# Keys, queries and values of a gated delta rule made token-major by VectorE block transposes and scattered stores, with norms taken per half, in a hybrid layer kernel

## The chip, the core and the metric

The kernel runs on one core of one Trainium2 chip. The metric is the device time of one execution in microseconds: the median of three runs, and beside it one profiled execution with its trace. Engines are named as in the profile: PE (TensorE matmuls), PEld (its weight loads), DVE (VectorE), ACT (ScalarE), POOL (GpSimd), SP (the queue that issues all DMAs here).

## The reference

One layer of a hybrid encoder trunk is computed for 2048 prompt tokens and 32 sample tokens, width 1024, in float32. The mixer projects the normalised input and splits the columns: half go through a spatial-gating MLP, half through a gated delta rule with 4 heads of 128. Then follow an output projection, and a feed-forward part with squared ReLU and 4096 hidden channels. What the change touches is this (shortened):

```python
qkv, new_buf = causal_conv(qkv, conv_buf, conv_w)
qkv = jax.nn.silu(qkv).reshape(B, L, 3 * DN_HEADS, DN_HEAD_DIM)
q = l2norm(qkv[:, :, :DN_HEADS]) * (DN_HEAD_DIM ** -0.5)
k = l2norm(qkv[:, :, DN_HEADS:2 * DN_HEADS])
vv = qkv[:, :, 2 * DN_HEADS:].astype(jnp.float32)
...
a = jnp.einsum('bhnid,bhnjd->bhnij', kb, k) * dec_strict
sol = triangular_solve(a + eye, concat([v * beta, kb * exp(gc)]), lower=True, unit_diagonal=True)
attn = jnp.einsum('bhnid,bhnjd->bhnij', q, k) * dec_incl
kg = k * jnp.exp(gc[..., -1:] - gc)[..., None]
...
v_new = u_i - w_i @ s
o = qg_i @ s + attn_i @ v_new
s = s * gl_i + kg_i.T @ v_new
```

## The kernel before, in words

The kernel keeps activations channel-major: 128 channels on the partitions, tokens along the columns. It does not write its instructions in a fixed order. Each operation is recorded with its engine, an estimated cost and what it reads and writes (`Program.op`), and `Program.schedule` then simulates the engines and writes a static list for each one. Among the operations that are ready an engine takes the one with the best priority (the recurrence first, then the inverse, the local work, evictions, and the large projections last), and by due time after that. A PSUM bank is a ring of its own for each kind of work: "g" for projections, "L" for local work, "C" for the recurrence, "B" for the inverse, "M" for the rest. On the chip each engine runs its list strictly in order, with semaphores. All DMAs go through SP, in order too.

The tokens are split into two halves of 1024 and 1056 columns (the 32 sample tokens are at the end of the second). For each half `mixers` runs these stages, whose matmuls the schedule mixes:

- `v_stage`: the gating MLP's v and the decay and beta columns, token-major; `gates` makes the decays.
- `qkv_tile`, once for each of k, q and v of each head: a projection per group of up to 512 tokens (24 matmuls, three per 128 rows of the contraction, for the split of a float32 in two), a copy of the bank to SBUF, a causal convolution of width 4 (one scaled copy on ACT, three operations on DVE), SiLU, and a store in DRAM: k and q of a head in `kq_d`, v in `v_d`.
- `delta_local`, once per head and half, in four batches of two chunks of 128 tokens. It loads k, q and v, turns each chunk on PE with the identity (line 431: six transposes a batch, into ring "L"), squares k and q out of PSUM on ACT with an accumulator read for the norms, takes a power of -1/2 on POOL, makes small columns from it, multiplies k with k and q (the score products, ring "L") and scales them by the decays. The turned and scaled k and v and the scaled scores go packed to `pk_d`.
- `delta_inv`, once per pair of heads and half: the inverse of the triangular matrices, by a solve on POOL and small matmuls in ring "B".
- `delta_chain`, once per pair: the recurrence over eight chunks of 128 tokens in ring "C". For each batch `load` brings packed k, v, scores, the inverse and k, q channel-major.
- `sample`: the same for the 32 sample tokens of all four heads; its results, like those of `delta_out`, pass through DRAM (`mix_d`).
- `u_stage`: the gating MLP's u.

Then `out_stage` projects the first half, and the second. Its input is loaded from `mix_d` and split in two (BH on ACT, BL on DVE). The feed-forward part follows in three blocks of tokens.

The lines that the page and the views name are those of helpers: L358 `act` (ACT), L373 `tt`, L378 `stt`, L387 `ts` (DVE or POOL), L396 `cp`, L404 the 32x32 block transpose of DVE (the view calls it STREAM_TRANSPOSE; before, it is used in the inverse alone), L411 `dma`, L420 a matmul, L431 a transpose on PE. Names like "s" are slots of SBUF, "L", "g", "C" the rings of banks, "wh" and "wl" the two parts of the weights.

## Time and profile before

| | |
|---|---|
| median of 3 runs | 2304.45 us (2303.17 to 2306.07) |
| profiled execution | 2305.26 us, its span 2303.5 us |
| mean granted TensorE clock | 0.998 |
| DMA, mean over the span | 238 GB/s, 547.32 MB |
| packets under 512 B | 66233 of 358198 |

A row of a group names line, engine, operation, what is written and read, shapes and count; then busy us in total and the mean ns of one instruction, and the idle time of the engine ahead of them with what ended it. A row of the order of time begins with the start and the duration in us from the span's start. Matmuls overlap, so the distance of two starts tells what one costs, rather than its duration. A row of one tile's or line's instructions gives the shortest, median and longest duration in ns.

### The profile page before, as it was taken

To read this page: it belongs to the slowest core of one execution; us is meant where nothing else is said; L and a number is where in the kernel's file an instruction comes from. 1 tells how busy PE (TensorE), PEld (TensorE's weight loads), DVE (VectorE), ACT (ScalarE), POOL (GpSimd) and SP (SyncE) were. 2 spreads that over 40 slices of the span, in tenths; PEclk is the share of its full clock that TensorE was granted. 3 is DMA by queue.
4 is the path that set the end of the run, shared out by engine and by line. 5 is a ranking of instruction groups with operands and counts; after the bars stand their busy time and mean duration, and the time that the engine had idled before them with its cause. 6 is when DMAs were issued, how large, how long until landed. Compare 5 with 4: busy or idle time off the path is not lost.

```text
span 2303.5 us, 45375 instructions
## 1 busy us (share of the span) xinstructions
PE 2280.8 (99%) x15890; PEld 2172.0 (94%) x15890; DVE 1660.0 (72%) x3599; ACT 1208.3 (52%) x2787; POOL 568.0 (25%) x722
## 2 busy tenths in 40 slices
PE   9999999999999999999999999999999999999998
PEld 6877879999999988999999999999999999999998
DVE  7556756677654546589999989876668885666775
ACT  5466656566654434476655546753444564344344
POOL 1123531222413023444445424210001250000001
PEclk9999999999999999999999999999999999999999
DMA  9578877576556857987777787997668797666771
GB/s 330 170 267 285 265 233 234 154 225 206 155 182 197 263 190 226 295 267 265 257 255 263 251 273 242 335 306 246 216 212 265 258 306 230 217 220 216 249 221 54
DMA packets 358198, 547.32 MB, mean 238 GB/s; under 512 B 66233, under 2 KB 182093, under 8 KB 357969
## 3 DMA queue, kind: packets, MB, share of 16 engines
q1 hardware_dynamic: 357968, 544.42, 72.6%
q8 instruction: 125, 2.05, 0.4%
q14 instruction: 105, 0.85, 0.1%
HBM read 390.96 MB, written 153.31 MB: 236 GB/s over the span
## 4 chain that ended last, share of the span: by engine, by line
PE 84%; DVE 6%; DMA 4%; ACT 2%; issue 2%; SPq 1%; POOL 1%; POOLq 0%; DVEq 0%; ACTq 0%
PE f L420 47%; PE g L420 27%; DVE s L373 4%; PE C L420 3%; PE B L420 2%; PE L L420 2%; DVE wl L373 1%; SPq L411 1%; ACT s L358 1%; PE M L420 1%; PE L L431 1%; DMA s<-x_d 1%; POOL s L373 0%; DMA s<-s_d 0%; ACT wh L358 0%
## 5 line engine op out<-in xcount | busy, mean ns | idle before, releaser
L420 PE MATMUL f<-s,wh 128*128 128x348 f32 (+1 forms) x2768 | 662.3, 322 | 1.3 <-DVE s L373 1.3
L358 ACT ACTIVATE s<-s 128x348 f32<-128x348 f32 (+13 forms) x1059 | 491.2, 487 | 326.6 <-DVE s L373 146.8
L420 PEld LDWEIGHTS f<-s,wh 128*128 128x128 f32 x2768 | 481.0, 188 | 3.3 <-DVE s L373 2.8
L373 DVE TENSOR_TENSOR s<-f,s 128x348 f32<-128x348 f32 (+1 forms) x696 | 348.0, 513 | 166.6 <-PE f L420 164.5
L420 PE MATMUL f<-s,wl 128*128 128x348 f32 (+1 forms) x1384 | 444.7, 321 | 0.0
L420 PE MATMUL g<-BH,wh 128*128 128x384 f32 (+2 forms) x1088 | 400.4, 368 | 2.4 <-ACT s L358 1.9
L373 DVE TENSOR_TENSOR s<-s,s 128x348 fp32r<-128x348 f32 (+8 forms) x674 | 353.2, 553 | 41.1 <-ACT s L358 20.5
L420 PE MATMUL g<-BH,wl 128*128 128x384 f32 (+2 forms) x1088 | 381.7, 351 | 0.0
L420 PE MATMUL g<-BL,wh 128*128 128x384 f32 (+2 forms) x1088 | 380.6, 350 | 0.5 <-DVE BL L378 0.5
L420 PE MATMUL f<-BL,wh 128*128 128x348 f32 (+1 forms) x1024 | 330.2, 322 | 0.0
L420 PE MATMUL f<-BH,wh 128*128 128x348 f32 (+1 forms) x1024 | 329.0, 321 | 0.0
L420 PE MATMUL f<-BH,wl 128*128 128x348 f32 (+1 forms) x1024 | 328.6, 321 | 0.0
L373 POOL TENSOR_TENSOR s<-s,s 128x512 f32<-128x512 f32 (+17 forms) x303 | 241.3, 800 | 341.2 <-ACT s L358 138.0
L358 ACT ACTIVATE wh<-s 128x512 fp32r<-128x512 f32 x282 | 176.6, 631 | 226.6 <-PE f L420 180.3
L420 PEld LDWEIGHTS f<-s,wl 128*128 128x128 f32 x1384 | 260.4, 188 | 0.0
L373 DVE TENSOR_TENSOR wl<-s,wh 128x512 fp32r<-128x512 f32 x282 | 217.2, 777 | 37.9 <-ACT wh L358 37.7
L420 PEld LDWEIGHTS g<-BH,wh 128*128 128x128 f32 x1088 | 204.9, 188 | 26.8 <-issue 7.1
L420 PEld LDWEIGHTS g<-BH,wl 128*128 128x128 f32 x1088 | 204.3, 188 | 18.2
L420 PEld LDWEIGHTS g<-BL,wh 128*128 128x128 f32 x1088 | 205.4, 189 | 16.6 <-DVE BL L378 0.8
L378 DVE SCALAR_TENSOR_TENSOR s<-s,s,s 128x256 f32<-128x256 f32 (+4 forms) x314 | 164.1, 544 | 55.3 <-ACT s L358 29.5
L358 ACT ACTIVATE wh<-wr 128x512 fp32r<-128x512 f32 (+2 forms) x159 | 124.3, 783 | 139.6 <-PE f L420 61.0
L420 PEld LDWEIGHTS f<-BL,wh 128*128 128x128 f32 x1024 | 192.3, 188 | 0.4 <-DVE BL L373 0.3
(134 smaller groups left out, 3264.6 us busy)
## 6 DMA issues: line engine op xcount, KB each, us to landing
s<-w_u SPq DMA_DIRECT2D x124, 256.0 KB, 3.6
s<-w_d SPq DMA_DIRECT2D x121, 256.0 KB, 3.9
wh<-su_d SPq DMA_DIRECT2D x114, 256.0 KB, 3.8
wl<-su_d SPq DMA_DIRECT2D x114, 256.0 KB, 4.1
wh<-sd_d SPq DMA_DIRECT2D x100, 256.0 KB, 3.0
wl<-sd_d SPq DMA_DIRECT2D x100, 256.0 KB, 3.8
wr<-w_b SPq DMA_DIRECT2D x36, 512.0 KB, 5.0
s<-adaw SPq DMA_DIRECT2D x32, 512.0 KB, 5.9
```

What stands on the lines that cost most here:

```text
L358: self.p.op(ACT, c, lambda: nc.scalar.activation(out=R(out), in_=R(in_), func=func, **{k: R(v) for k, v in kw.items()}), [out, accum], [in ...
L373: self.p.op(eng, c, lambda: e.tensor_tensor(out=R(out), in0=R(a), in1=R(b), op=op), [out], [a, b])
L378: self.p.op(DVE, c, lambda: nc.vector.scalar_tensor_tensor(out=R(out), in0=R(a), scalar=R(s), in1=R(b), op0=op0, op1=op1), [out], [a, s, b])
L411: self.p.op(DMA, max(500, x), lambda: nc.sync.dma_start(out=R(out), in_=R(in_)), [out], [in_], lat=LAND + b / RATE - max(500, x))
L420: nc.tensor.matmul(R(out), R(l), R(r), **kw)
L431: self.p.op(PE, 114, lambda: nc.tensor.transpose(R(out), R(in_), R(ident)), [out], [in_, ident])
```

## The change

k, q and v are turned on DVE, in `qkv_tile`, once the whole half of a tile has gone through SiLU into one buffer `yo` of 1056 columns. One block transpose turns 32x32 blocks: it reads columns 33 apart, so that a block holds the tokens i*33 + c of 32 channels, and writes contiguous columns to `yt`. For k and v four DMAs (one for each 32 channels) then store the blocks token-major in `kt_d`, as 1056 pieces of 32 elements each. For k and q, `yt` is squared in place on ACT, summed over the 32 channels of each piece on DVE (`sums`), and stored in `ns_d` as partial sums of squares.

`delta_local` loads the four partial sums of k and q of a head's whole half at once, turns them with one transpose on PE (64 rows, ring "B"), adds them, and makes the norm columns for all eight chunks together. The six transposes a batch, the squares with accumulators and the scaled copies of k and v go from there; it stores only the scores. `delta_chain`'s `load` now reads k and v from `kt_d`, 1 KB a token, and scales them in place on ACT with the same columns. The score products still read channel-major k and q. `sample` reads token-major k and v from `kt_d` and its partial sums from `ns_d`.

Beside that, the slabs of weights come in the order k, q, k, q, v, v for each pair of heads; a head's `delta` is called behind its q instead of its v. The first scaled copy of the convolution reads the SBUF copy, not the bank. Ring "g" has three banks, "L" one. The normalisation of the second half's input is given a due time.

```diff
-        self.banks = {"g": [0, 1], "L": [3, 2], "C": [4, 5], "B": [6], "M": [7]}
+        self.banks = {"g": [0, 1, 2], "L": [3], "C": [4, 5], "B": [6], "M": [7]}
...
+            self.p.due = len(self.p.ops) + 300 * (g + 1)
...
-            fm = ["k0", "q0", "v0", "k1", "q1", "v1", "k2", "q2", "v2", "k3", "q3", "v3"]
+            fm = ["k0", "q0", "k1", "q1", "v0", "v1", "k2", "q2", "k3", "q3", "v2", "v3"]
...
-                        if name[0] == "v":
+                        if name[0] == "q":
                             self.delta(hf, int(name[1]))
+                        elif name[0] == "v":
                             due.append(int(name[1]))
...
-            raw, y, yo = self.new("raw"), self.half("y", w), self.half("yo", w)
+            raw, y, yo = self.new("raw"), self.half("y", w), self.yo[:, o : o + w]
...
-            self.act(y, ps, AF.Identity, scale=cw(3))
+            self.act(y, raw[:, 3 : 3 + w], AF.Identity, scale=cw(3))
...
             self.act(yo, y, AF.Silu)
-            self.dma(dst[:, T0[hf] + o : T0[hf] + o + w], yo)
+            if ty < 2:
+                self.dma(self.kq_d[h][:, 1 - ty, T0[hf] + o : T0[hf] + o + w], yo)
+        self.transpose32(self.yt.re("p (c j) -> p c j", j=32), self.yo.re("p (i c) -> p c i", i=32))
+        if ty:
+            for b in range(4):
+                self.dma(self.kt_d[h][hf][:, ty - 1, 32 * b : 32 * b + 32].re("(i c) j -> i c j", i=32), self.yt[32 * b : 32 * b + 32].re("p (c j) -> p c j", j=32), 2 * P * SLOT)
+        if ty < 2:
+            self.act(self.yt, self.yt, AF.Square)
+            part = self.new("sqp")
+            self.sums(part, self.yt.re("p (c j) -> p c j", j=32))
+            self.dma(self.ns_d[h][hf][1 - ty].re("b (i c) -> (b i) c", i=32), part)
...
+        ns, rr = self.new("ssl"), self.new("ssr")
+        self.dma(ns[:64], self.ns_d[h][hf][:, :, :TW[0]].re("x b (c p) -> (x b) c p", p=P))
+        ss, rr = rr[:, :16], rr[:, 16:]
+        pt = self.bank("B")
+        self.tr(pt[:, :64], ns[:64], self.ident[:64, :64])
+        self.sums(ss.re("p (x c) -> p x c", x=2), pt[:, :64].re("p (x b c) -> p x c b", x=2, b=4))
+        self.ts(ss, ss, EPS, ALU.add)
+        self.rsqrt_small(rr, ss)
...
-            self.dma(vt[:, :W], self.v_d[h][:, t0 : t0 + W])
...
-            pt = self.bank("L")
-            for x in range(2):
-                for e in range(n):
-                    o = 256 * x + 128 * e
-                    self.tr(pt[:, o : o + 128], kq[:, x, wide(e)], self.ident)
-            for x in range(2):
-                for e in range(n):
-                    o = 256 * x + 128 * e
-                    jk = self.new("jk")
-                    self.act(jk[:w], pt[:w, o : o + 128], AF.Square, accum=ss[:w, n * x + e : n * x + e + 1])
-            for e, c in enumerate(cl):
-                self.act(pk[:w, 1, 128 * e : 128 * e + 128], pt[:w, 128 * e : 128 * e + 128], AF.Copy, scale=self.ekg[:w, h, c : c + 1])
...
-            pv = self.bank("L")
-            for e in range(n):
-                self.tr(pv[:, 128 * e : 128 * e + 128], vt[:, wide(e)], self.ident)
-            for e, c in enumerate(cl):
-                s = slice(128 * e, 128 * e + 128)
-                self.act(pk[:w, 2, s], pv[:w, s], AF.Copy, scale=nk[:w, e : e + 1])
-            self.dma(self.pk_d[h][b], pk)
+            self.dma(self.pk_d[h][b], at)
...
+            self.dma(kv, self.kt_d[h][hf][lt : lt + W].re("(e p) x j -> p e (x j)", e=n))
+            self.dma(us, self.us_d[h][hf][:, P * lc : P * lc + W])
+            self.dma(at, self.pk_d[h][b])
             self.dma(kq, self.kq_d[h][:, :, t0 : t0 + W])
+            for e, c in enumerate(cl):
+                for x, k in enumerate((self.ekg, self.nk)):
+                    v = kv[:, e, P * x : P * x + P]
+                    self.act(v, v, AF.Copy, scale=k[:, h, c : c + 1])
```

The static lists change throughout the mixers. Two places on PE matter to what follows. Lines are those of each kernel: a transpose is L431 before and L433 now, a matmul L420 and L422.

The first batch of head 0 in the first half, before, between two matmuls of a projection (L: the bank for local work, s: k and q as loaded):

```order
L420 MATMUL g_2248<-BL_79,wh 128x512
L420 MATMUL g_2248<-BH_71,wl 128x512
L431 MATMUL L_1098<-ident,s_470 128x128 [waits DMAHW6_49]
L431 MATMUL L_1098<-ident,s_470 128x128 x3
L420 MATMUL L_1152<-s_470 128x256 x2
L420 MATMUL g_2248<-BH_72,wh 128x512
L420 MATMUL g_2248<-BL_80,wh 128x512
```

The same place now:

```order
L422 MATMUL g_2197<-BL_86,wh 128x512
L422 MATMUL g_2197<-BH_78,wl 128x512
L422 MATMUL L_1164<-s_482 128x256 [waits DMAHW3_49]
L422 MATMUL L_1164<-s_482 128x256
L422 MATMUL g_2242<-BH_71,wh 128x512
L422 MATMUL g_2242<-BL_79,wh 128x512
```

The four transposes of k and q are gone (those of v stood further on), and the two score products stand alone between projections.

The end of the mixers, before: the transpose of the sample's result (into C) in the first half's output projection. The third group of the second half, 288 columns wide, needs that result in BH_75 and the three behind it; its first matmul on BH_75 is 176 rows further down the list:

```order
L420 MATMUL g_10216<-BL_82,wh 128x512
L420 MATMUL g_10216<-BH_74,wl 128x512
L431 MATMUL C_10243<-ident,s_469 128x128 [waits DVE_49,PE_49]
L420 MATMUL g_10216<-BH_75,wh 128x512
L420 MATMUL g_10216<-BL_83,wh 128x512
```

Now the same transpose stands inside that third group of the second half itself:

```order
L422 MATMUL g_10127<-BL_80,wh 128x288 [waits DVE_49]
L422 MATMUL g_10127<-BH_72,wl 128x288
L433 MATMUL C_10171<-ident,s_481 128x128 [waits DVE_49,PE_49]
L422 MATMUL g_10127<-BH_73,wh 128x288
L422 MATMUL g_10127<-BL_81,wh 128x288
```

and PE comes back to the group for BH_75 behind a tile of 384 columns from the next slab:

```order
L422 MATMUL g_10220<-BH_78,wh 128x384
L422 MATMUL g_10220<-BL_86,wh 128x384
L422 MATMUL g_10220<-BH_78,wl 128x384
L422 MATMUL g_10127<-BH_75,wh 128x288 [waits Activation_49]
L422 MATMUL g_10127<-BL_83,wh 128x288 [waits DVE_49]
L422 MATMUL g_10127<-BH_75,wl 128x288
```

Between the sample's transpose and the first matmul on its result stand 42 rows: six and twelve matmuls of 288 columns and 24 of 384. The two tiles of the group are left at half their contraction and taken up again.

97 lines of the change are left out of this document (51 added, 46 removed).

## The prediction

> **What bounds the kernel now.** I read the page's busy shares first, then the busy time by stretch, then who TensorE (PE) waited for, then the order of time around the instructions that go.
>
> ```profile
> span 2303.5 us, 45375 instructions
> PE 2280.8 (99%) x15890; PEld 2172.0 (94%) x15890; DVE 1660.0 (72%) x3599; ACT 1208.3 (52%) x2787; POOL 568.0 (25%) x722
> ```
>
> PE is busy for 2280.8 of 2303.5 us. The change lies in the mixers, so the next view cuts the span at 140 us (first transposes of keys), 720 us (end of the last inverse) and 960 us (start of the feed-forward part). Its columns are us of the stretch, then the busy us of each engine with its instructions, then clock, DMA share and GB/s.
>
> ```profile
> 140.00:720.00 580.00, 576.40 (x4717) 520.88 (x4716) 379.30 (x1094) 346.80 (x988) 185.41 (x382) 1.00 0.70 219
> 720.00:960.00 240.00, 238.61 (x1805) 216.53 (x1805) 136.07 (x306) 99.17 (x223) 68.55 (x83) 1.00 0.74 232
> 960.00:2303.00 1343.00, 1331.16 (x8373) 1326.94 (x8372) 1061.38 (x2011) 692.71 (x1440) 293.58 (x227) 1.00 0.75 246
> ```
>
> In the 580 us that hold all the turned work, PE idles 3.6 us, while DVE is busy for 65% and ACT for 60%. PE's own waits in that stretch are these (total, times, longest):
>
> ```profile
> PE g L420 <- ACT s L358: 1.9, 3, 0.9
> PE L L431 <- ACT s L358: 1.0, 1, 1.0
> ```
>
> So the time there is the length of PE's list, and an instruction that leaves it is a gain unless a new wait appears. PE runs strictly in the written order, so a new wait of PE is paid in full.
>
> **What leaves PE.** Line 431 in the ring "L" is the group of transposes that goes: six per batch, 32 batches, and three of the sample.
>
> ```profile
> L431 PE MATMUL L<-ident,s 128*128 128x128 f32 x195 | 28.8, 274 | 1.0 <-ACT s L358 1.0
> ...
> 201.71 0.60 PE L431 MATMUL L<-ident,s 128*128 128x128 f32 x4
> 202.15 1.03 PE L420 MATMUL L<-s 128*128 128x256 f32 x4
> ...
> 227.08 0.39 PE L420 MATMUL g<-BH,wl 128*128 128x512 f32 x1
> 227.31 0.82 PE L431 MATMUL L<-ident,s 128*128 128x128 f32 x6
> 227.89 0.48 PE L420 MATMUL g<-BH,wh 128*128 128x512 f32 x1
> 228.21 0.40 PE L420 MATMUL g<-BL,wh 128*128 128x512 f32 x1
> 228.44 0.39 PE L420 MATMUL g<-BH,wl 128*128 128x512 f32 x1
> ```
>
> The mean of 274 ns is a latency: instructions overlap, so I go by the distance of starts. A projection matmul of 512 columns is followed by the next after 0.23 us (228.21 to 228.44). From the first of six transposes (227.31) to the second projection matmul behind them (228.21) pass 0.90 us; less one 0.23 that leaves 0.67, or 0.112 us each, with the slow return to projections included. Four in a row ahead of other L work take 0.44 us, 0.110 each. The term is 195 x 0.112 = **-21.8 us** (at 0.110: -21.5). The group's 28.8 us busy is no better guide, since that union counts tails under which the next matmul already runs.
>
> Eight new transposes of a [64, 128] tile come to PE (one per head and half), at most as dear as the old ones: 8 x 0.11 = **+0.9 us** (up to 1.6 if each also pays its own slow return).
>
> **What moves to DVE, ACT and POOL.** None of this is on the path by itself; it counts only where PE waits for it.
>
> ```profile
> L404 DVE STREAM_TRANSPOSE s<-s x9: 205/711/712, 315.1 to 743.9; 128x512 f32<-128x512 f32 x8, 128x32 f32<-128x32 f32 x1
> L373 DVE TENSOR_TENSOR s<-s 128x2 f32<-128x2 f32 x128 | 19.2, 176 | 21.5 <-POOL s L373 19.2 <-ACT s L358 1.9
> L358 ACT ACTIVATE s<-L 128x128 f32<-128x128 f32 x130 | 36.6, 281 | 4.5 <-PE L L431 3.0
> L358 ACT ACTIVATION_READ_ACCUMULATOR s<-L 128x1 f32 x130 | 27.1, 209 | 0.0
> L358 ACT ACTIVATE s<-s 128x1024 f32<-128x1024 f32 x8 | 8.5, 1062 | 0.9 <-DVE s L378 0.9
> L373 POOL TENSOR_TENSOR s<-s,mhalf 128x4 f32<-128x4 f32 x32 | 34.6, 1081 | 94.3 <-DVE s L387 92.1 <-DVE s L378 2.0
> L373 POOL TENSOR_TENSOR s<-s,mhalf 128x2 f32<-128x2 f32 x33 | 24.0, 731 | 86.3 <-DVE s L373 41.1 <-ACT s L358 33.2 <-DVE s L387 12.1
> ```
>
> DVE's block transpose takes 205 ns for 32 columns and 711 for 512, 1.05 ns a column, so 1056 columns should take 1.28 us: 24 of them are 31 us. The 16 sums over 1056 elements have no row; taken like the transposes they are 20 us. About 160 small operations (five a batch) at 0.17 us shrink to some 48, so 19 us go. DVE gains 32 us on 379 of 580, from 65% to some 71%. ACT loses 128 squares with their accumulator reads, 128 x 0.49 = 63 us, and gains 16 squares of about 1.09 us, 17 us. Its 128 scaled copies remain but move to the loads of the recurrence. On POOL 32 powers of 1.08 us become eight; by the step from two to four columns, 0.175 us a column, 16 columns take 3.2 us. Cover is there on all three engines: none is over 71% in the stretch.
>
> The third bank for projections and the single read of each bank should take away part of the waits shown above (1.9 us on ACT; the 1.0 us in front of a vanished transpose goes by itself): **-1.5 us**, between 0 and -2.9. One bank instead of two for the score products, which now stand alone and apart, I price at nothing; what covers it is the projection tile (24 x 0.23 = 5.5 us) that usually lies between two of them. Without that cover it costs a few tenths each.
>
> **The stores.** A tile of k or v is stored by four DMAs of 1056 pieces of 128 bytes. Per head and half, eight of these and three norm transfers come in, and the v stores, v loads and two thirds of the packed stores go out. Behind a store in the SP queue wait all loads, the weights' among them; behind the in-place square on ACT, which needs the four stores landed, wait the copies that free projection banks; behind the sum on DVE, the next tile's transpose. The nearest rows for scattered stores:
>
> ```profile
> L411 SPq DMA_DIRECT2D ud_d<-s x18: 303/484/642, 84.2 to 717.2; - x18
> ...
> DMA to landing us min/median/max: 1.7/1.9/4.0
> ...
> L411 SPq DMA_DIRECT2D s<-eye x5: 333/2322/2954, 88.9 to 719.8; - x5
> ```
>
> Sixteen of the ud_d stores have 512 pieces of 64 bytes: 0.48 us to issue, 1.9 to land, at most 4.0. Twice the pieces should be near 1 us to issue and 2 to 4 to land, so four are done 6 to 7 us after the transpose. A tile has 11.1 us of projections (48 x 0.23), and 1.28 + 7 + 1.09 + 1.28 = 10.7 us fit into it. I take **+1.0 us** for scattered short waits, between 0 and 6: near the low end, as the scattered rows are the closest.
>
> [...]
>
> **The end of the mixers.** With the norms ahead of the scores, and the slabs in another order, the recurrences stand later in PE's list. The last one's tail, the sample's transpose, stands 176 rows ahead of the first projection matmul that needs its result before, and 42 rows ahead now: six and twelve matmuls of 288 columns and 24 of 384. At 0.23 us per 512 columns (0.13 and 0.17) that is 18 x 0.13 + 24 x 0.17 = 6.5 us of cover. The path it has to cover is seen here:
>
> ```profile
> 877.51 0.27 PE L431 MATMUL C<-ident,s 128*128 128x128 f32 x1
> 877.83 0.35 DVE L378 SCALAR_TENSOR_TENSOR s<-C,s,s 128x128 f32<-128x128 f32 x1 [0.28 <-PE C L431]
> ...
> 878.20 1.75 SPq L411 DMA_DIRECT2D mix_d<-s  x4
> ...
> DMA to landing us min/median/max: 1.5/3.8/6.2
> ...
> L358 ACT ACTIVATE BH<-s 128x288 fp32r<-128x288 f32 x16 | 6.6, 448 | 3.6 <-DMA s<-mix_d 3.6
> L373 DVE TENSOR_TENSOR BL<-s,BH 128x288 fp32r<-128x288 f32 x16 | 6.8, 454 | 5.1 <-ACT BH L358 5.1
> ```
>
> From the transpose to the first store issue 0.7 us, a store and a load through mix_d at 3.8 each, then 0.45 on ACT and 0.45 on DVE, with some 0.3 between: 9.5 us. Less 6.5 of cover, PE waits **+3.0 us** once; with the landings' ends (1.5 and 6.2) it is 0 to 8.
>
> **Sum.** The profiled execution took 2305.26 us, 1.8 outside its span, and lies 0.8 above the median of three, 2304.45. 2305.3 - 21.8 + 0.9 - 1.5 + 1.0 + 3.0 = 2286.9; less 0.8, **2286 us**. All low ends give 2305.3 - 21.8 + 0.9 - 2.9 - 0.8 = 2281, all high ends 2305.3 - 21.5 + 1.6 + 6 + 8 - 0.8 = 2299. About 0.2%, 4.6 us, is what a measurement of this kernel can tell from no change: faster is below 2299.8, slower above 2309.
>
> **The rivals.**
>
> First, DVE is slower than its row. The transposes of the trace read contiguous columns; the new ones read elements 33 apart. If that doubles them, DVE has 31 us more. The twelve of the first half precede most of the recurrence and would hide; the twelve of the second share DVE with it, and each could hold up a step for which PE stands ready, by up to 1.28 us: 0 to 15 us, half of it 8, **2294**. For it: no row reads at such a stride. Against it: DVE has 29% idle. Chance 0.14.
> [...]
>
> Second, the delay reaches the end. A head's scores now wait for transpose, square, sum, a store, a load, a small transpose and a power: 1.28 + 1.09 + 1.28 + 3.8 + 3.8 + 0.3 + 3.2 = 14.8 us. If the list's order doesn't hide that for the last pair of heads, all of it comes on top of 2286 as waits of PE from the last inverse on: **2301**, no difference. For it: the 42 rows of cover. Against it: PE has projections for over 100 us in between. Chance 0.10.
>
> Third, on the other side: the stores hold the turned tile. If the issue of 1056 pieces is like the eye row's 2.3 us, four take 9.2 and land 4 later, 13.2 us. A v tile then holds its one buffer for 14.5 us, two in a row 29, against 22.2 of projections: 6.8 over, in four pairs 27 us, **2313**, slower. It becomes slower than before when four stores take some 12.7 us (5.8 over in each pair). For it: SP issues in order, and one buffer. Against it: the 512-piece rows. Chance 0.07.
>
> Fourth, the transposes ran where PE would have waited anyway, so that nothing is gained: 2304. Against it stands the 3.6 us of idle. Chance 0.03.
>
> **How the numbers follow.** My forecast, 2286 with its own range of 2281 to 2299, has 0.66. With the first rival (0.14) and 0.01 of the second, where a part of the delay is covered, faster has 0.81. No difference has the rest of the second and the fourth, 0.12; slower the third, 0.07. The range of 2279 to 2300 takes in the forecast and the first rival, with 2 us below the low ends for the spread of runs, and leaves out 0.19.
>
> **What would show it.** No L transposes on PE, its busy time in the mixers some 21 us lower, and idle there of no more than 10 us. A DVE transpose of 1.28 us (2.6: the first rival). Four stores landing within 7 us of it (13: the third). One wait of PE for ACT or DVE of about 3 us ahead of the first projection matmul with the sample's rows, near 890 us (18: the second). The feed-forward part should take the 1343 us that it takes now; a change there would make the argument wrong, as would a PE that idles over 20 us in the mixers.

## The result and the profile after

The changed kernel takes 2317.88 us (median of four runs, 2313.77 to 2325.33), the kernel before 2305.26 in the same comparison (2303.17 to 2306.77): ratio 1.0059, interval 1.0032 to 1.0086. It is slower by 12.6 us where 18 us less were forecast. The profiled execution took 2325.33 us, the longest of the four, with a span of 2323.6; sums from the trace are of that one.

The page of the changed kernel, busy times of the engines and DMA packets:

```profile
PE 2276.7 (98%) x15703; PEld 2159.8 (93%) x15703; DVE 1704.0 (73%) x3528; ACT 1197.5 (52%) x2547; POOL 554.9 (24%) x699
...
DMA packets 431793, 539.69 MB, mean 232 GB/s; under 512 B 137528, under 2 KB 264908, under 8 KB 431568
```

The 195 transposes are gone, and still PE is busy only 4.1 us less than the 2280.8 of before. Its idle time rose from 22.7 us (2303.5 less 2280.8) to 46.9 (2323.6 less 2276.7), 24.2 more: 24.2 - 4.1 is the 20.1 us by which the span grew. From the first matmul of the feed-forward part to the end of the span both traces take 1315 us, so everything lies in the mixers. The longest of PE's waits there (engine and what it waited for: us in total, times, longest):

```profile
PE L L422 <- DMA s<-kq_d: 4.6, 6, 1.6
PE B L422 <- DVE s L406: 4.1, 4, 2.4
PE g L422 <- ACT BH L360: 3.6, 2, 2.0
PE B L422 <- DVE s L375: 3.5, 1, 3.5
PE L L422 <- issue: 3.4, 3, 1.6
PE C L422 <- ACT s L360: 2.8, 3, 1.7
PE g L422 <- DVE wl L375: 2.0, 1, 2.0
```

No single long wait has come in. The rows shown hold twenty short ones, for loads (kq_d), for DVE and for ACT; "issue" means that the view names no releaser. The new operations, by form (busy us, mean ns), then the token-major stores (min, median and max ns of an issue on SP):

```profile
L406 DVE STREAM_TRANSPOSE s<-s 128x1056 f32<-128x1056 f32 x24 | 51.9, 2164 | 4.4 <-ACT s L360 2.7 <-DMA kt_d<-s 1.4
L1194 DVE TENSOR_REDUCE s<-s 128x33 f32<-128x1056 f32 x16 | 20.0, 1248 | 5.0 <-ACT s L360 4.9
L406 DVE STREAM_TRANSPOSE s<-s 128x512 f32<-128x512 f32 x8 | 5.7, 707 | 4.2 <-DMA s<-ud_d 4.1
```

```profile
L413 SPq DMA_DIRECT2D kt_d<-s x64: 561/742/3817, 182.2 to 663.3; - x64
...
DMA to landing us min/median/max: 1.6/4.0/6.6
```

A block transpose that reads elements 33 apart takes 2.16 us, not 1.28; the contiguous form of 512 columns still takes 0.71. The sums are as forecast. The landing row covers only 16 transfers, loads of kt_d among them; by the semaphores in the trace, the counters that a landing raises, the 64 stores land 3.8 us after their issue begins, in the median, which is as forecast for one store. But the 64 issues, 0.74 us in the median, add up to 59.6 us of SP's time. Between 140 and 900 us SP is busy issuing for 431 us, against 354 before (durations of its rows added up). How that reaches PE is seen on SP's queue, then on DVE, PE and ACT, at 255 to 274 us:

```profile
255.08 0.60 SPq L413 DMA_DIRECT2D kt_d<-s  x1
256.75 4.63 SPq L413 DMA_DIRECT2D kt_d<-s  x3
261.42 1.98 SPq L413 DMA_DIRECT2D s<-xT  x3
263.50 0.38 SPq L413 DMA_DIRECT2D kq_d<-s  x1
...
264.96 0.41 SPq L413 DMA_DIRECT2D wr<-w_b  x1
...
268.04 5.57 SPq L413 DMA_DIRECT2D kt_d<-s  x3
```

```profile
264.44 2.15 DVE L406 STREAM_TRANSPOSE s<-s 128x1056 f32<-128x1056 f32 x1 [1.40 <-DMA kt_d<-s]
266.93 0.61 DVE L380 SCALAR_TENSOR_TENSOR s<-L,s,s 128x128 f32<-128x128 f32 x2
267.64 1.10 PE L422 MATMUL L<-s 128*128 128x256 f32 x4 [1.59 <-issue]
268.27 0.63 ACT L360 ACTIVATE s<-s 128x512 f32<-128x512 f32 x1 [6.67 <-DMA kq_d<-s]
```

Three stores hold the queue for 4.6 us, the next three for 5.6, and whatever stands behind them goes out late. The four stores of one tile, which was turned at 250.87, go out from 255.08 to 261.37. The next transpose needs the same buffer `yt` and waits 1.40 us for them to land. It takes 2.15 us, and behind it in DVE's list stand the operations that read the last score products out of ring "L". The next score products need that bank, since the ring has only one: PE's weight load for them begins 0.07 us after the last read, at 267.61, and PE has waited 1.59 us. The other two waits that the view calls issue, 0.41 us at 259.37 and 1.45 at 275.76, end 0.07 us behind such a read as well. Ahead of the one at 275.76 DVE had waited for the high part of a weight slab (wh), whose load went out at 264.96, behind the three stores. The next score products, at 288.18, wait 1.56 us for their own load of k and q. ACT stands for 6.67 us until a store of k or q that went out behind them has landed.

The stride shows on DVE at 309 to 322 us:

```profile
309.30 1.25 DVE L1194 TENSOR_REDUCE s<-s 128x33 f32<-128x1056 f32 x1 [2.24 <-ACT s L360]
310.59 2.17 DVE L406 STREAM_TRANSPOSE s<-s 128x1056 f32<-128x1056 f32 x1
312.69 1.18 DVE L375 TENSOR_TENSOR wl<-wr,wh 128x1024 fp32r<-128x1024 f32 x1
314.44 1.25 DVE L1194 TENSOR_REDUCE s<-s 128x33 f32<-128x1056 f32 x1 [0.57 <-ACT s L360]
315.61 0.74 DVE L380 SCALAR_TENSOR_TENSOR s<-s,s,s 128x512 f32<-128x512 f32 x1
316.27 2.19 DVE L406 STREAM_TRANSPOSE s<-s 128x1056 f32<-128x1056 f32 x1
...
320.89 1.21 DVE L375 TENSOR_TENSOR wl<-wr,wh 128x1024 fp32r<-128x1024 f32 x1
```

DVE works through its list nearly without a gap, and the low part of a weight slab, last in this row, is ready at 322.1. PE waits for it, and for what comes after, here in PE's timeline and in the table of stretches (the column behind POOL's is PE's granted clock):

```profile
322.16 0.50 PE L422 MATMUL g<-BH,wl 128*128 128x512 f32 x1 [2.01 <-DVE wl L375]
...
341.22 0.72 PE L422 MATMUL B<-s,s 32*32 32x16 f32 x64 [2.38 <-DVE s L406]
351.53 1.05 PE L422 MATMUL B<-s,s 32*32 32x16 f32 x64 [3.50 <-DVE s L375]
```

```profile
316.00:322.00 6.00, 4.14 (x18) 3.01 (x16) 6.00 (x9) 2.64 (x6) 2.07 (x2) 1.00 0.45 93
322.00:327.00 5.00, 4.84 (x14) 3.86 (x15) 3.12 (x6) 4.94 (x6) 4.61 (x11) 0.66 0.87 226
327.00:332.00 5.00, 5.00 (x23) 4.03 (x23) 4.56 (x8) 2.26 (x4) 0.61 (x4) 1.00 0.86 198
346.00:351.00 5.00, 2.03 (x58) 1.39 (x46) 0.98 (x2) 1.12 (x2) 0.00 (x0) 0.96 0.97 316
351.00:358.00 7.00, 6.47 (x78) 5.28 (x79) 3.76 (x7) 6.48 (x13) 0.00 (x0) 0.54 0.93 282
```

Behind a wait of 2.01 us the clock is at half for 3.4 us; at the one of 3.50 us a stretch of 6.8 begins. In the first, 14 matmuls stand in 5 us where the next 5 us hold 23. In all the changed kernel has 20.5 us at half clock ahead of its last microseconds, the kernel before none. Up to 10 us of PE's busy time are that, half of the 20.5 as an estimate: without it the busy time would have fallen by up to 14 us and not by 4.

### The profile page after: what moved, and what is told of

The parts are those of the page before. It is cut to its first block, busy times and chain, and to the rows that moved or that the text cites. A ratio compares the mean times of both kernels' runs of the same rounds, so it can differ in the third digit from the quotient of the medians.

```text
span 2323.6 us, 44705 instructions
## 1 busy us (share of the span) xinstructions
PE 2276.7 (98%) x15703; PEld 2159.8 (93%) x15703; DVE 1704.0 (73%) x3528; ACT 1197.5 (52%) x2547; POOL 554.9 (24%) x699
## 4 chain that ended last, share of the span: by engine, by line
PE 51%; DVE 2%; issue 1%; POOL 1%; ACT 1%; DMA 0%; SPq 0%; POOLq 0%; DVEq 0%; ACTq 0%
PE f L422 51%; DVE s L375 1%; POOL s L375 1%; ACT s L360 1%; DVE wl L375 1%; DMA s<-w_u 0%; DVE s L380 0%; DMA s<-x_d 0%; ACT wh L360 0%; PE M L422 0%; PE M L433 0%; SPq L413 0%; DVE BL L375 0%; POOL wr L375 0%; ACT BH L360 0%
## 5 line engine op out<-in xcount | busy, mean ns | idle before, releaser
L360 ACT ACTIVATE s<-s 128x348 f32<-128x348 f32 (+13 forms) x1075 | 505.9, 495 | 335.7 <-DVE s L375 152.0
L422 PE MATMUL f<-s,wh 128*128 128x348 f32 (+1 forms) x2768 | 662.4, 322 | 1.9 <-ACT s L360 1.3
L422 PEld LDWEIGHTS f<-s,wh 128*128 128x128 f32 x2768 | 480.6, 188 | 3.8 <-ACT s L360 1.9
L422 PE MATMUL f<-s,wl 128*128 128x348 f32 (+1 forms) x1384 | 444.7, 321 | 0.0
L422 PE MATMUL g<-BH,wh 128*128 128x384 f32 (+2 forms) x1104 | 409.1, 371 | 4.5 <-ACT BH L360 3.6
L422 PE MATMUL g<-BH,wl 128*128 128x384 f32 (+2 forms) x1104 | 390.3, 354 | 2.0 <-DVE wl L375 2.0
L422 PE MATMUL g<-BL,wh 128*128 128x384 f32 (+2 forms) x1104 | 391.0, 354 | 0.6 <-DVE BL L380 0.5
L375 DVE TENSOR_TENSOR s<-s,s 128x348 fp32r<-128x348 f32 (+9 forms) x650 | 350.8, 569 | 48.9 <-ACT s L360 23.0
L422 PE MATMUL f<-BH,wh 128*128 128x348 f32 (+1 forms) x1024 | 330.0, 322 | 0.7 <-DVE s L375 0.7
L422 PE MATMUL f<-BL,wh 128*128 128x348 f32 (+1 forms) x1024 | 329.2, 321 | 0.0
L375 POOL TENSOR_TENSOR s<-s,s 128x512 f32<-128x512 f32 (+18 forms) x303 | 244.2, 810 | 355.1 <-ACT s L360 168.6
L422 PE MATMUL f<-BH,wl 128*128 128x348 f32 (+1 forms) x1024 | 328.9, 321 | 0.0
L422 PEld LDWEIGHTS f<-s,wl 128*128 128x128 f32 x1384 | 260.5, 188 | 0.0
L422 PEld LDWEIGHTS g<-BH,wh 128*128 128x128 f32 x1104 | 209.9, 190 | 31.4 <-issue 6.7
L422 PEld LDWEIGHTS g<-BH,wl 128*128 128x128 f32 x1104 | 209.9, 190 | 22.3 <-DVE wl L375 2.4
L422 PEld LDWEIGHTS g<-BL,wh 128*128 128x128 f32 x1104 | 209.9, 190 | 17.8 <-DVE BL L380 0.8
L422 PEld LDWEIGHTS f<-BH,wh 128*128 128x128 f32 x1024 | 192.4, 188 | 1.2 <-ACT wh L360 1.0
L422 PEld LDWEIGHTS f<-BH,wl 128*128 128x128 f32 x1024 | 193.0, 188 | 0.0
```

Of the source, the lines that this page charges most:

```text
L360: self.p.op(ACT, c, lambda: nc.scalar.activation(out=R(out), in_=R(in_), func=func, **{k: R(v) for k, v in kw.items()}), [out, accum], [in ...
L375: self.p.op(eng, c, lambda: e.tensor_tensor(out=R(out), in0=R(a), in1=R(b), op=op), [out], [a, b])
L422: nc.tensor.matmul(R(out), R(l), R(r), **kw)
```

## The experiments

All were compared with the kernel before; "after's lists" means that the order of instructions on every engine is that of the changed kernel.

| kernel | lists | us, median | ratio to before, interval |
|---|---|---|---|
| changed kernel | own | 2317.88 | 1.0059, 1.0032 to 1.0086 |
| e1_unit: contiguous reads | after's | 2310.96 | 1.0026, 1.0016 to 1.0036 |
| e2_few: stores in 32 pieces | after's | 2306.8 | 1.0002, 0.9992 to 1.0012 |
| e3_both: both | after's | 2297.87 | 0.9960, 0.9946 to 0.9974 |
| e9_ready_e3: both, norms always ready | after's | 2299.66 | 0.9966, 0.9953 to 0.9979 |
| e10_ready: norms always ready | after's | 2320.89 | 1.0057, 1.0038 to 1.0076 |
| e17_pool: stores from GpSimd's queue | after's | 2428.46 | 1.0535, 1.0507 to 1.0563 |
| e14_dve: before, 18.7 us more on DVE | before's | 2308.91 | 1.0007, 0.9997 to 1.0017 |
| e15_pieces: before, 64 scattered stores | before's | 2337.27 | 1.0127, 1.0112 to 1.0142 |
| e8_gap: before, 24 waits of PE | before's | 2414.53 | 1.0474, 1.0453 to 1.0495 |
| e4_cost: planned with the true cost | new | 2323.07 | 1.0080, 1.0065 to 1.0095 |
| e5_sqyo: squares elsewhere | new | 2317.78 | 1.0056, 1.0039 to 1.0073 |
| e6_unit: contiguous reads, norms that follow | new | 2319.55 | 1.0063, 1.0047 to 1.0079 |
| e7_unit_sqyo: both of these | new | 2318.07 | 1.0056, 1.0041 to 1.0071 |
| e16_e7few: e7 with stores in 32 pieces | e7's | 2301.4 | 0.9975, 0.9965 to 0.9985 |
| e18_pool_e7: e7, stores from GpSimd's queue | e7's | 2413.73 | 1.0461, 1.0441 to 1.0481 |
| e11_banks: banks as before | new | 2326.69 | 1.0084, 1.0067 to 1.0102 |
| e12_nodue: no due times | new | 2331.56 | 1.0107, 1.0089 to 1.0125 |
| e13_order: slabs as before | new | 2310.36 | 1.0010, 1.0001 to 1.0020 |

The profile left three suspects: the stride on DVE (the first rival of the prediction), the scattered stores (the third), and the planner, which did not know the true durations.

**The stride alone, the pieces alone, both.** In after's lists, one edit each; beside it a large constant stands in the place of EPS, and k, v or the norms stand at other tokens than the reference's:

```diff
-self.transpose32(self.yt.re("p (c j) -> p c j", j=32), self.yo.re("p (i c) -> p c i", i=32))
+self.transpose32(self.yt.re("p (c j) -> p c j", j=32), self.yo.re("p (c i) -> p c i", i=32))
```

> The changed kernel (2317.9 us, before 2305.3) with one edit: the block transpose reads contiguous columns, not columns 33 apart; all lists are the same. The norms then sit at other tokens, so 1e4 stands in the place of EPS beside the sums of squares to keep the recurrence bounded (same instructions). Theory A, the stride: the transposes of 2.15 us fall to 1.28, PE's new waits behind DVE and the half-clock stretches that follow them mostly go: 2287 to 2296 us. Theory B, the scattered stores hold ACT and SP: transposes fall, but PE waits as before: 2312 to 2318. Theory C, the new list itself is at fault: the same, 2310 to 2318.

```diff
-self.dma(self.kt_d[h][hf][:, ty - 1, 32 * b : 32 * b + 32].re("(i c) j -> i c j", i=32),
-         self.yt[32 * b : 32 * b + 32].re("p (c j) -> p c j", j=32), 2 * P * SLOT)
+r = 132 * (4 * (ty - 1) + b)
+d = self.kt_d[h][hf][r : r + 132].re("r x j -> (r x j)").re("(i m) -> i m", i=32)
+nc.sync.dma_start(out=d, in_=self.yt[32 * b : 32 * b + 32])
```

> The changed kernel with the four stores of k and v as 32 pieces of 4224 bytes each, not 1056 of 128 bytes; same bytes, same lists, values at other places in kt_d, and the same constant beside the sums. Theory A: transposes stay at 2.15 us, 2312 to 2318 us. Theory B: the issue on SP falls from 0.74 to about 0.35 us, ACT's 25 us of waits for these stores go, 2288 to 2298 us. Theory C: 2310 to 2318.

> Both edits at once, contiguous reads and 32-piece stores, same lists. Theory A: hardly better than contiguous reads alone, 2285 to 2295 us. Theory B: hardly better than the large pieces alone, 2286 to 2298. If both share: 4 us or more below the better single one. Theory C: still above 2305.

Contiguous reads: 2310.96 us, 7 less than the changed kernel. Fewer pieces: 2306.8, 11 less. Both: 2297.87, 20 less and 9 below the better single one, so both share and the two about add up. Theories A and B had each taken the whole loss: the stride is out as the only cause by e1, and the stores by e2, which lies between the ranges. Theory C, the new list, would have allowed e1, but expected e3 above 2305. With both edits the transposes are, by form,

```profile
L406 DVE STREAM_TRANSPOSE s<-s 128x1056 f32<-128x1056 f32 x24 | 30.6, 1273 | 3.0 <-ACT s L360 2.7
```

and with fewer pieces alone the store rows read

```profile
L1188 SPq DMA_DIRECT2D kt_d<-s x64: 302/421/1034, 180.0 to 644.1; - x64
```

The same 64 DMAs with the same bytes take 29.0 us of SP's time, not 59.6. By the semaphores they land 2.9 us after their issue begins, not 3.8, but 2.5 after it ends, not 2.8. PE's waits for kq_d went from 4.6 us to 0.3, and the three waits for the bank of ring "L" are gone.

**The planner, told the true cost.**

```diff
-self.p.op(DVE, 68 + 1.042 * out.n, lambda: nc.vector.transpose(R(out), R(in_)), [out], [in_])
+self.p.op(DVE, 2150 if out.n == SLOT else 68 + 1.042 * out.n, lambda: nc.vector.transpose(R(out), R(in_)), [out], [in_])
```

> The changed kernel, correct as it is, with one number changed in its schedule: 2150 ns, as measured, for a block transpose of 1056 columns where it had 1168; the lists are written anew. Theory A in the form that DVE's time itself is the trouble: no better, 2312 to 2320 us. Theory A in the form that the lists were written for a transpose that is 1 us too short: 2290 to 2302. Theory B: no better, 2312 to 2320.

2323.07 us, a little over the first range: knowing the duration does not help, and a new list by itself moved the time by 5 us. Differences of that size between separately planned lists mean little.

**Who waits for the stores.** Squares that go to another tile, contiguous reads with norms that follow, and both together:

```diff
-self.act(self.yt, self.yt, AF.Square)
-self.sums(part, self.yt.re("p (c j) -> p c j", j=32))
+self.act(self.yo, self.yt, AF.Square)
+self.sums(part, self.yo.re("p (c j) -> p c j", j=32))
```

> The changed kernel, with one difference: the squares for the norms go to the tile yo, which is free after the block transpose, and not in place into yt. So ACT's square no longer waits for the four token-major stores to land (24.8 us of ACT waits in the changed kernel); the stores and their issue on SP stay as they are. The planner writes new lists. Theory A, the small pieces cost time because the square waits for their landing: the 9 to 11 us that fewer pieces gave come back, 2305 to 2311 us. Theory B, they cost time because their issue holds SP's queue and the loads behind it: no gain, 2314 to 2322 us, and PE's waits for the loads of kq_d stay near 4.6 us. Lists alone have moved the time by 5 us.

```diff
+self.sums(part[:, :32].re("p (r c) -> p c r", r=4), self.yt[:, :1024].re("p (c r j) -> p c r j", r=4, j=32))
...
-self.dma(ns[:64], self.ns_d[h][hf][:, :, :TW[0]].re("x b (c p) -> (x b) c p", p=P))
-pt = self.bank("B")
-self.tr(pt[:, :64], ns[:64], self.ident[:64, :64])
+for r in range(4):
+    self.dma(ns[32 * r : 32 * r + 32, :64].re("p (y c) -> p y c", y=8), self.ns_d[h][hf].re("x b (t m) -> t (x b) m", t=32)[:, :, 8 * r : 8 * r + 8])
```

> The changed kernel with block transposes that read contiguous columns, and norms that follow the new order of tokens: the sums are written in four groups of eight columns, stored once and loaded by four DMAs of 256 pieces of 32 bytes, so that they come token-major by themselves and the small transposes of 64 x 128 on PE go too. The computation is the reference's. Theory A, the stride of 33 is one of the two causes: transposes of 1.27 us and about 7 us less than the changed kernel, 2308 to 2313 us. Theory B, what was seen with the contiguous read hung on its lists alone: no gain with new lists, 2315 to 2324 us.

> The two differences before this one together: contiguous reads with norms that follow, and squares into yo. The computation is the reference's. If stride and landing are the two causes and add up: 2297 to 2304 us, faster than the kernel before. If the issue on SP, and not the landing, is the second cause: 2308 to 2313 us. If every new list loses some 15 us in waits whatever the durations are: 2312 to 2324 us.

> The kernel with contiguous reads and squares into yo (2318.1 us) with its own lists, and its token-major stores in 32 pieces of 4224 bytes each, the same bytes laid out otherwise in memory, so that the recurrence reads k and v in a wrong order; all instructions and waits stay. Theory A, the scattered stores hold SP's queue in this list too, and are all that is left of the loss: 2296 to 2304 us. Theory B, this list has waits of its own: 2309 to 2318 us.

The first three lie at 2318 to 2320 us, as if nothing had been mended. For e5 theory B came in, and its expectation had misread a row: the 24.8 us of ACT's waits are almost all for the recurrence's loads of kt_d, 23.1 us, and not for the stores ahead of the square. For e6 and e7 the range for lists that lose whatever the durations are came in (they also load the norms in 36 transfers instead of 12, 12 to 13 us more of SP's time, so they do not test the stride alone), until the stores of e7 were put in 32 pieces: 2301.4 us, 17 less and faster than before. So the stores cost in this list what they cost in after's, and more.

**The price of each by itself, on the kernel before.**

```diff
+o = [o for o in self.p.ops if o.eng == DVE][-1]   # one a tile
+f, j = o.fn, self.junk
+o.fn = lambda: (f(), nc.vector.scalar_tensor_tensor(out=R(j), in0=R(j), scalar=..., in1=R(j), ...))
```

> The kernel before with its own lists, and 24 more operations of VectorE of 0.75 us on a tile of their own that nothing reads, one behind the convolution of each q, k and v tile, 18 us in all: the price of VectorE's time alone, about the 21 us that the stride adds. Theory A, the lists leave no slack on VectorE's in-order queue, and any longer operation reaches PE by what stands behind it: 4 to 8 us slower, 2309 to 2314 us. Theory B, VectorE's 35% of idle time covers it, and the stride cost what it did only in the changed kernel's lists: within 2 us of before, 2303 to 2307 us.

```diff
+for b in range(4 if ty else 0):   # behind the tile's last store
+    nc.sync.dma_start(out=R(d[:, ty - 1, 32 * b : 32 * b + 32].re("(i c) j -> i c j", i=32)), in_=...)
```

> The kernel before with its own lists, and behind the stores of each k and v tile four more stores of 1056 pieces of 128 bytes from a small constant tile to memory that nothing reads, 64 in all: the price of the scattered stores' issue and traffic alone, with nothing that waits for them to land. Theory A, SP's in-order queue, at 0.74 us each 47 us in all, delays the loads behind it: 8 to 14 us slower, 2313 to 2320 us. Theory B, what costs is who waits for their landing (the squares and the next transpose): within 3 us of before, 2303 to 2308 us.

DVE's time alone costs 0.7 parts in a thousand, 1.6 us, with an interval that holds zero: before's lists have the slack, and theory B's "within 2 us of before" came in (2308.91 lies between the two ranges, but before itself was 2307.83 in this comparison). The stores alone cost 29.3 us (0.0127 x 2307.83), over twice what theory A said; their issues took 72.5 us of SP's time and not 47. Nothing reads what they write, and nothing waits for them but SP's own queue. The kernel's own transfers behind them are late, as ACT's waits for one of them show, the packed stores whose buffer ACT refills; before, then with the 64 stores:

```profile
ACT s L358 <- DMA pk_d<-s: 12.3, 10, 3.9
```

```profile
ACT s L358 <- DMA pk_d<-s: 30.3, 15, 4.4
```

DVE's waits for the same stores went from 2.5 to 20.2 us, while the median landing of pk_d moved only from 3.0 to 3.5 us. Over all of the kernel's own transfers from 140 to 900 us whose landing the trace tells, the mean from issue to landing is 3.74 us before (390 of them) and 3.78 with the 64 stores (367): once issued they are no slower in the mean (medians: loads of kq_d 4.3 and then 3.5, weights w_b 5.1 and 5.4), so most of the lateness lies ahead of the issue, in the queue. PE is idle 16.1 us more than before, and busy 12.6 us more, with 27.3 us at half clock.

**The same pieces from another queue.**

```diff
-self.dma(self.kt_d..., self.yt..., 2 * P * SLOT)
+self.dma(self.kt_d..., self.yt..., 2 * P * SLOT, self.nc.gpsimd)
```

> The changed kernel with its own lists, and the 64 token-major stores issued from GpSimd's queue instead of SP's: the same pieces, bytes, order and waits. Theory A, what costs is the time that their issue takes in SP's in-order queue (60 us, and loads stand behind it): at least what fewer pieces gave, 2298 to 2309 us. Theory B, what costs is the pieces themselves, on the DMA engines or in their landing: within 4 us of 2317.9. Theory C, GpSimd's own issue takes long and holds the small powers and copies behind it: slower than 2321 us.

> The kernel with contiguous reads, norms that follow and squares into yo (2318.1 us), with its own lists, and the 64 token-major stores issued from GpSimd's queue. The computation is the reference's. If SP's queue is what is left of the loss, as the store in few pieces said (2301.4 us): 2296 to 2304 us, faster than the kernel before. If the pieces cost wherever they are issued: 2314 to 2321 us.

For e17 theory C came in, far beyond its bound: 111 us slower than in SP's queue. In e7's list it is 96, outside both ranges of e18. The store rows of e17 on GpSimd, and what PE waited for longest:

```profile
L414 POOL DMA_DIRECT2D kt_d<-s x64: 773/783/984, 177.5 to 776.8; - x64
its engine sat idle before it (us, times) until:
  issue: 146.5, 46
```

```profile
PE M L434 <- POOL rcol L375: 20.6, 3, 10.9
PE g L423 <- ACT s L360: 16.4, 6, 7.1
PE B L423 <- DVE s L406: 14.5, 2, 8.9
PE M L423 <- POOL s L375: 13.6, 1, 13.6
```

An issue takes 0.78 us, but 46 of the 64 had 3.2 us ahead of them in which GpSimd did nothing and waited for nothing that the profile shows, and the small copies and powers of the mixers stand in that queue. So this run does not tell the issue from the traffic of the pieces as it was meant to. It does show again that an in-order queue, held at 64 places, is paid for by PE: its four rows hold 65.1 us.

**The norms' path.** In after's lists the load of a head's norms reads a weight tensor, so that nothing there waits for transpose, square, sum and store; without and with the two edits of e3:

```diff
-in_=self.ns_d[h][hf][:, :, :TW[0]]
+in_=self.i["w_b"][0, :64, :P]
```

> The changed kernel (strided transposes, stores of 1056 pieces, same lists) with the norms loaded from a weight tensor that is always ready, in place of where they were stored; all instructions stay, the values of the norms are wrong. Theory A, the norms' path is the carrier through which slow transposes and stores reach PE: most of the 20 us that both of them cost goes, 2298 to 2306 us. Theory B, they reach PE through the in-order queues of DVE, ACT and SP, by copies that free projection banks and by loads: within 5 us of the changed kernel's 2317.9.

> The kernel with contiguous block transposes and stores in few pieces (same lists as the changed kernel), and in it a head's norms no longer loaded from where they were stored but from a weight tensor, which is always ready: the load, the small transpose, the sum and the power stay, but nothing in them waits any more for the head's transposes, squares, sums and their store. The norms' values are wrong thereby (a large constant is added so that they stay positive). Theory A (the second rival of the prediction, moved to the end of the first half): the norms' path through memory is late for the last heads of a half, and PE's waits of 300 to 360 us and 700 to 780 us in this kernel hang on it: 5 to 9 us less than its 2297.9, 2289 to 2293 us. Theory B: those waits come from in-order queues and the rest of the list: within 2 us of 2297.9.

2320.89 and 2299.66 us, against 2317.88 and 2297.87: no gain in either. Theory B in both: the long path of the norms through memory is not what PE pays for.

**Parts of the change undone.** Banks, due times, order of the slabs:

```diff
-self.banks = {"g": [0, 1, 2], "L": [3], ...}
+self.banks = {"g": [0, 1], "L": [3, 2], ...}
```

> The changed kernel with the banks as before: two for projections and two for the score products, instead of three and one. New lists. If the single bank for score products makes PE wait (waits of L for a load or for PE's sequencer were 8 us in the changed kernel): 2306 to 2313 us. If the third bank for projections helped as forecast: 2319 to 2325 us.

```diff
-self.p.due = len(self.p.ops) + 300 * (g + 1)
```

> The changed kernel without the due times on the second half's statistics (one line of the change taken out). New lists. If pulling the statistics of the second half forward, into 240 to 360 us where the last heads of the first half end, makes the waits there (18 of the 34 us of stalls more than before lie there): 2303 to 2311 us. If the due times were needed, because the second half's projections otherwise wait for the statistics: 2322 to 2340 us. If they do not matter: 2313 to 2321 us.

```diff
-fm = ["k0", "q0", "k1", "q1", "v0", "v1", "k2", "q2", "k3", "q3", "v2", "v3"]
+fm = ["k0", "q0", "v0", "k1", "q1", "v1", "k2", "q2", "v2", "k3", "q3", "v3"]
```

> The changed kernel with the slabs in the order of before: k, q, v of a head, then the next head (weights laid out to match), the score products still behind q. New lists. If the order kkqqvv of a pair, with its v tiles last, is what leaves PE short of work at the end of the first half: 2303 to 2312 us. If it is neutral: 2314 to 2322 us. If it was needed, since it gives a head's norms more time: 2322 to 2335 us.

With the banks as before the changed kernel is 9 us slower, a little over its second range, and without due times 14; as far as one list each can tell, it needs both parts. With the slabs in before's order it is 8 us faster, 2310.36, as the first range said: the best of the kernels here that do the whole computation with token-major k and v, and 0.1% behind the kernel before. These are single lists each, so of their sizes only those well over 5 us are to be trusted.

**What a wait costs.** Deliberate waits in the feed-forward part of the kernel before:

```diff
 for k, (out, l, r, kw) in enumerate(calls):
+    for _ in range(n if k == 0 else 0):   # n = 2, 4, ... 12, every 80th group
+        nc.vector.tensor_copy(R(r), R(r.f32()))
     nc.tensor.matmul(R(out), R(l), R(r), **kw)
```

> The kernel before, with 24 deliberate waits of PE in the feed-forward part, far from each other: ahead of every 80th group of three matmuls VectorE copies the group's moving operand onto itself (values are unchanged) 2, 4, 6, 8, 10 or 12 times, at some 0.25 us each, so that PE waits about 1.0, 1.5, 2.0, 2.5, 3.0 and 3.5 us, four times each: 54 us of waits in all. Theory A, a wait of PE of 2 us or more is followed by 3.4 us at half the granted clock, which costs 1.7 us more: 16 of the 24 waits pay it, 27 us, and the time is 2380 to 2392 us; after waits of 1.5 us or less matmuls keep their 0.16 us spacing. Theory B, the halved stretches of the changed kernel had another cause: 2355 to 2364 us, and no row of PE's clock below 0.97 in the feed-forward part.

The copies were slower than assumed, so the waits are longer; PE's two rows for them:

```profile
PE f L428 <- DVE BH L427: 42.5, 12, 6.1
PE f L428 <- DVE s L427: 34.8, 12, 4.7
```

They add up to 77.3 us, and the kernel became 109.4 us slower: 32 us more than PE waited. One of the waits in PE's timeline, and the stretches around it:

```profile
1252.56 0.66 PE L428 MATMUL f<-BH,wh 128*128 128x348 f32 x1 [5.48 <-DVE BH L427]
```

```profile
1246.00:1252.00 6.00, 1.08 (x7) 0.80 (x6) 5.66 (x12) 0.63 (x1) 2.85 (x3) 0.94 0.50 168
1252.00:1258.00 6.00, 5.44 (x19) 5.44 (x20) 2.55 (x7) 1.95 (x4) 0.00 (x0) 0.50 0.27 87
1258.00:1264.00 6.00, 6.00 (x38) 6.00 (x37) 5.67 (x10) 3.35 (x8) 1.30 (x1) 0.99 0.51 175
```

Behind the wait 19 matmuls take 5.4 us, where the next 6 us hold 38. The clock record of the feed-forward part holds 15 such stretches, nine of 3.4 us and six of 6.8, 71.7 us, which cost up to 36 by the same estimate. By PE's idle time: all 13 waits of 3.2 us and more brought one, two of the eight between 1.9 and 2.7 us, none of the three of 1.4 us and less. This is theory A with the length of the waits put right, but not its limit of 2 us; theory B would have given 2305 + 77 = 2382.

What the halving goes with is seen when all 20 traces are cut into steps of 3.413 us that fit the beginnings of the halved stretches to some 5 ns (the first 20 and the last 40 us of each left out). At full clock there are 70 steps in which PE idled 1.9 us or more, and a halved stretch followed all of them. It followed 21 of 145 steps with 1.0 to 1.9 us of idle time, and one of some 12900 with less: the stretch at 466.6 us of the changed kernel, ahead of which, back to 352 us, PE's longest wait was 0.34 us. Why that one came is open. So it matters where a wait falls: in e13 one of 3.53 us at 323.5 us is split into 1.66 and 1.87 us by two steps, and nothing followed.

## Why the prediction was wrong

**What the removal gave: sized too high.** The transposes went, but 16.8 us of the busy time that should have gone with them (20.9 forecast, 4.1 measured) did not. Up to 10.2 of it are the 20.5 us at half clock. The other 6.6 are the size of the term: with few halved stretches e3 is busy 11.2 us less than before (2269.6), 16.3 with its own 10.2 us at half clock taken out, so the removal was worth 14 to 16 us and not 21 (13.6 by the same sum in e2, 14.8 in e1). By the distance of starts the 195 transposes took 19.1 us before, not 21.8, and the eight new ones take 1.6, not 0.9; the other 3 us or so are spread over the remaining groups.

**The scattered waits: the step that failed.** "I take +1.0 us for scattered short waits, between 0 and 6" stands against 24.2 us more of idle time (2.5 with the other terms). The working behind it let the four stores of a tile be done 6 to 7 us after the transpose, so that square and sum fit into the tile's projections. A single store comes as forecast (0.74 us of issue, 3.8 to landing). But the four stand among other transfers in SP's queue: by the trace's semaphores the last one lands 8.0 us after the transpose in the median of the 16 tiles, from 5.7 to 24.3. Little waits for them directly (ACT 1.7 us, DVE 1.4). What costs more is what stands behind them in the queue, which the prediction named and gave no price. That price is the larger cause: 11 us of the changed kernel go when the issues take 29 us of SP and not 60 (e2), 13 us by the comparison of e1 with e3, 17 in another list (e16), and 29 come when the same stores are put into the kernel before (e15).

**One bank for the score products** was priced at nothing, for a tile of projections would lie between two of them. PE waited 3.4 us for that bank in the changed kernel, in the three waits shown as issue; with fewer pieces (e2) these waits go.

**The third rival** had the right operation, and its mechanism is the smaller part. It wanted four stores to take 13.2 us while the one buffer is held. Three of the 16 tiles took 13.0, 14.0 and 24.3 us, but DVE waited for the buffer only once, for 1.4 us, and taking the square's wait away (e5) gained nothing. The time from the end of the issue to landing hardly differs (2.8 us with pieces of 128 bytes in the changed kernel, 2.5 with 4224 in e2), and what differs is the issue, 0.74 us against 0.42. That PE pays for the queue and not for the traffic is the reading that fits e2 and e15 best, with the kernel's other transfers landing as fast as before in e15; the run meant to prove it (e17) could not.

**The first rival came true in its cause and size, though not in its place.** 24 transposes at 2.16 us: 7 us by e1, 9 by the step from e2 to e3, against its 8. But it had the first half's transposes hide and the second half's cost; of the 16.6 us that e1's profiled run is ahead of the changed kernel's, with the same order on PE, 9.5 come between 140 and 360 us. That its 8 us fit is in part luck. The forecast gave it a chance of 0.14 because DVE had 29% idle. That reason holds in before's lists, where 18.7 us more of DVE cost nothing measurable (e14), and not in the changed kernel's, where sums, transposes and weight splits follow each other in bursts as at 309 to 322 us. That the stride doubles a transpose was the author's assumption; the traces show 2.16 us at stride 33 (changed kernel) and 1.27 at stride 1 (e3), a factor of 1.7.

**The second rival did not come.** With the norms ready at any time nothing was gained (e9, e10).

**The end of the mixers** was forecast as a wait of 3.0 us and is there, 1.65 us at 936 us for ACT's BH; a halved stretch of 3.4 us follows it.

**The third bank** was priced at -1.5 us. Giving it back to the score products cost 9 us in a new list (e11), so the trade of banks was worth more in this one, and the direction was right.

**What no step had: the clock.** The prediction priced a wait at its length. A wait that puts 1.9 us or more of idle time into one step of the grid was followed by half clock every time, in 70 steps of 70, and a shorter one sometimes, in 21 of 145 with 1.0 to 1.9 us; each 3.4 us of it can add 1.7, half of it as an estimate. The kernel before has no wait above 1.54 us in the mixers, and no halved stretch there.

**The account.** In the profiled executions the forecast was 2286.9 and 2325.33 came, 38.4 more: 16.8 of PE's busy time (up to 10.2 of it the clock) and 21.7 of idle time. In medians, stride and pieces together are 20 of the 32 us. The other 12, by which e3 still lies above the forecast, are of the same two kinds: some 5 us each of too high a saving and of half clock, and 4 us of waits. Which wait of these belongs to which part of the change is not settled, since each test of it needs a newly planned list.

## What to carry to other kernels

Where one in-order queue issues all transfers, price a DMA by the time that its issue holds that queue and by what stands behind it, not only by when it lands: 30 us more of SP's time cost PE 11 to 17 us here, though the stores themselves were waited for only 3.1 us, by ACT and DVE. In a kernel that is 99% bound by PE, work taken off PE is worth less than its time as soon as it fills the queues that feed PE (here 19.1 us of transposes went, and the kernel became 12.6 us slower), and an engine's mean idle share does not say whether it has slack at the place that counts (DVE idled 27% of the changed kernel's span, and contiguous reads still gained 7 us). Price a wait of PE near two microseconds or more with the half clock that can follow it, as it did here behind the waits of 2.01 and 3.50 us.

## What the runs showed of the hardware

- PE's granted clock was halved in stretches of 3.4 us or whole multiples of it, which began on a fixed grid of 3.413 us: in the changed kernel at 323.27, 350.58, 466.63 and 937.67 us from the span's start, the later three 8, 42 and 180 steps behind the first; in e8 the first three at 619.86, 1073.83 and 1118.20 us, the later two 133 and 146 steps behind the first. In the changed kernel waits of 1.65 and 2.01 us were followed by a halved stretch, while six of the eight between 1.9 and 2.7 us in e8 and one of 3.53 in e13 were not. In all 20 traces it followed every step of the grid at full clock with 1.9 us or more of idle time, 70 of them.
- A 32 x 32 block transpose of 1056 columns of f32 takes 1.27 us when it reads contiguous columns (e3) and 2.16 us when it reads with a stride of 33 (changed kernel).
- The issue of a store of 135 KB on SP takes 0.42 us in the median in 32 pieces (e2) and 0.74 us in 1056 pieces, at most 3.8 (changed kernel).
- The same store issued by GpSimd takes 0.78 us (e17), and the engine stood still for 3.2 us on average ahead of 46 of the 64.
